# Attention heads in groups of two even and two odd ones, with their products issued in turn

## The chip, the cores and the metric

The program runs on one core of a Trainium2 chip. The metric is the device time of one execution in microseconds. A core has five engines with a queue of their own each: TensorE (PE, matmuls and transposes through a matmul with the identity; its weight loads are listed as PEld), VectorE (DVE), ScalarE (ACT), GpSimd (POOL) and SyncE (SP, which issues the weight loads from memory). An engine takes its instructions in the order in which the program issued them and waits on semaphores for the others.

## The reference

Two small models run one after the other on 256 tokens of 1024 channels. The first has two layers of a hybrid mixer (gated delta rule, retention, pooling) and a gated feed-forward. The second, with which this case deals, has two layers of a mixer with three attentions, a, b and c, and a feed-forward with squared relu. All heads are 64 wide, all arithmetic is float32.

```python
def hybrid_mixer_2(u, pos, w_in, idx_k_norm, sinks, w_a, w_b, w_c, w_o):
    (aq, ak, av, iq, ik, iw, bq, bk, bv, cq, ck, cv, gates) = split_columns(u @ w_in)
    ...
    o_a = dsa_attention(qa, ka, av, iqr, ikr, iw * IDX_HEADS ** -0.5)   # 6 heads, one k and v; 8 index heads
    o_b = dilated_attention(...)   # 4 heads in each of 3 groups; the softmaxes of the groups join
    o_c = sink_window_attention(..., sinks)   # 8 heads over 2 k and v heads, a sink logit in the softmax
    g = jax.nn.sigmoid(gates.reshape(Bsz, L, N_BRANCHES, D_MODEL))
    merged = (g[:, :, 0] * (o_a.reshape(Bsz, L, -1) @ w_a)
              + g[:, :, 1] * (o_b.reshape(Bsz, L, -1) @ w_b)
              + g[:, :, 2] * (o_c.reshape(Bsz, L, -1) @ w_c))
    return merged @ w_o
```

In attention a, 8 index heads give a score to each key, and only the best 64 keys of a row count.

## The kernel before

The tokens are two tiles of 128, t = 0 and t = 1. Tile 0 sees 128 keys, tile 1 sees 256 (`nk`).

**The main stream.** Products with weight matrices (`Block`, `unit`, `unit_b`, run by `run_blocks`) follow each other on PE in an order that is fixed when the program is built. Weights come by SP into `raw`; ACT copies them to `hi` (the part that the fast float32r format holds exactly), DVE subtracts to get `lo`, and each product is three matmuls: hi, lo and the rest of x with hi. Results go to four PSUM banks named `acc`; blocks that feed a feed-forward and all the small work use four others, named `sd`.

**The chains.** Everything else (norms, rope, attention) is written as Python generators, called chains. A chain yields the number of `sd` banks that its next step takes, or an event to wait for. While the program is built, the main stream calls `tick` after every few matmuls. A planner in the same code (`Engine.cost`, `mm`, `tr`, `op`) keeps an estimated clock for each engine, and lets a chain issue its next step when its operands are estimated to be ready. So the planner decides at which place of PE's order a chain's small products stand. On the chip the order is fixed, and a product whose operand is late holds up all that stands behind it on PE.

**The attentions.** `lane` (one chain for each token tile) runs `index_bias`, then the three attentions through `softmax_pv`. Queries and keys are transposed, two heads to a tile: an even head lies at partitions 0 to 63, an odd one at 64 to 127. The operands are `iqT`, `ikT` (index), `qaT`, `kaT` (a), `b1`, `b2`, `b3` (b), `c1`, `c2`, `ckT` (c); `av`, `bv1`, `bv2` and `cv` are the values. A unit is one head of b, or two heads of equal parity of a or c. `unit_pv` makes a unit's scores in a bank, DVE scales them and adds the mask into a tile `L`, finds the maximum `mx`; ACT takes the exponential and sums it into `den`; DVE divides; PE transposes `L` (128 columns at a time) and ACT copies the result to `PT`; then PE multiplies the values with `PT` into the attention's output bank, `po`: an even head at output partitions 0 to 63, an odd one at 64 to 127. `softmax_pv` takes up to two units of a token tile in flight: it waits for the unit before the last (`evs[-2]`) ahead of each new one. `split_T` then brings the output to `oT`, for the branch products of the main stream.

**In the order.** The units of the attentions before are `[[0, 2], [1, 3], [4], [5]]` for a, `[[0], [1], [2], [3]]` for b and `[[0, 2], [1, 3], [4, 6], [5, 7]]` for c. The products of a unit stand one behind the other, so those of one parity stand together.

Of the kernel before, what the change touches and what calls it, by code (L numbers as in the profile page):

```python
# [9 lines left out]
F32 = mybir.dt.float32  # L10
# [7 lines left out]
LEAD, RING = 8, 6  # L18
# [10 lines left out]
class Engine:  # L29
    """an engine's instructions, with an estimate of when each is done"""  # L30
# [43 lines left out]
class Chain:  # L74
    """g: generator; held: what its last step has yet to issue; r: what that step yielded; fin: when it is done"""
# [25 lines left out]
class Pair:  # L101
    """[128, 4, hi/lo, 256 tok] as two tiles of the arena"""
# [8 lines left out]
    def cuts(s, t, nk):  # L111
        """the first nk rows of token tile t, for split_T"""
        return [s.t[k // 2][:, 0:min(2, nk - k), :, t * 128:(t + 1) * 128] for k in range(0, nk, 2)]


class Net:
# [105 lines left out]
    def keys(s, a):  # L222
        """the parts of a tile, 128 elements each, that an access touches"""
# [6 lines left out]
    def when(s, ins, outs, lat=0.13):  # L230
        """when the operands of an instruction are ready"""
# [20 lines left out]
    def moved(s, t, mb, at=0.0):  # L252
        """a tile that a DMA fills, not before at"""
# [79 lines left out]
    def loads(s, n=3):  # L333
        """issue loads as far ahead as the buffers reach"""
# [13 lines left out]
    def hi(s, fine=False):  # L348
        """the high parts of the next piece, if there is room; fine: at most 512 columns of them"""
# [39 lines left out]
    def lo(s, fine=False):  # L389
        """the low parts of the next piece"""  # L390
# [20 lines left out]
    def hiready(s, fine=False):  # L411
        """when the high parts that the next low parts take are there"""
# [7 lines left out]
    def back(s, i):  # L420
        """how much work an engine may have before it when part of piece i is added"""
# [20 lines left out]
    def slack(s, i):  # L442
        """time that the tensor engine has to work before it takes piece i"""
# [20 lines left out]
    def unit(s, b, pi, t, half=None):  # L464
        """half: of the columns of kind "d", else both"""
# [90 lines left out]
    def ar(s, shape, name, dt=F32, kb=0):  # L556
        """a tile of the arena: slots of 1, 2 and 4 KiB a partition"""
# [50 lines left out]
    def rstd(s, parts, n):  # L608
        """(sum of the columns of parts / n + 1e-6) ** -0.5"""
# [14 lines left out]
    def split_T(s, cuts, ps):  # L624
        """the rows of ps [128, n, 128] in two parts; cuts: where they go, in [128, n, hi/lo, 128]"""
# [7 lines left out]
    def to_T(s, cuts, src):  # L633
        """transposes src [128 tok, nk*128], nk <= 4"""
# [9 lines left out]
    def norm_T(s, t, ss, w, ev):  # L644
        """xT of rms_norm(x[t]) * w; ss: sums of squares of the two halves"""
# [15 lines left out]
    def add_normed(s, t, acc, w, ns, ev):  # L661
        """x[t] += rms_norm(acc) * w, acc two banks, ev: the second is done; ns: sums of squares of the new x[t]"""
# [23 lines left out]
    def acc(s):  # L686
        """accumulators of kind "d", [t][half], taken when they are first used"""
# [148 lines left out]
class Mix1:  # L836
# [28 lines left out]
    def rope_tm(s, dst, src, cos, sin, nsin, nh, half):  # L865
        """dst, src [128, nh, 2, half]; tables [128, half]"""
# [8 lines left out]
    def branch_blocks(s, st, oT, ev, w, K, gt, first, done=None):  # L875
        """y += (1 + gt) * (o @ w), transposed: twice the gated sum; done: the split of y into xT"""
# [21 lines left out]
    def gate_blocks(s, w, c0, need):  # L898
        """tanh of half of 1024 columns (sigmoid is half of 1 + it), transposed; gt[half][pair of 128 columns]"""
# [17 lines left out]
    def out_bank(s, aT, v, q, sts):  # L917
        """[128 tok, head, dv]: a @ v plus each chunk's q @ (state before it)"""
# [29 lines left out]
    def decay(s, st, ba):  # L948
        """beta, running sums of the log decay and their exponentials"""
# [8 lines left out]
        # softplus(u) = max(u, 0) + log1p(exp(-|u|)); log1p(e) = 2 atanh(e / (2 + e))  # L958
# [33 lines left out]
    def conv(s, st, b):  # L992
        """evacuation of 128 transposed columns: causal convolution along the tokens, silu"""
# [17 lines left out]
    def delta(s, st, t):  # L1011
        """gated delta rule of one token tile (two chunks of 64), four heads side by side"""
# [10 lines left out]
        # inverse norms of the rows of q and k  # L1023
# [10 lines left out]
        # decay matrices  # L1034
# [32 lines left out]
        # attn^T  # L1067
# [11 lines left out]
        # (I + M)^-1 by doubling the diagonal blocks  # L1079
# [30 lines left out]
        # u and w^T  # L1110
# [48 lines left out]
        # attention inside the chunks, then what the states add  # L1159
# [131 lines left out]
    def mixer1(s, l, need, finish):  # L1291
        """blocks of one layer's mixer and what to do at its start"""
# [104 lines left out]
class Mix2:  # L1397
    def load_consts2(s):
# [4 lines left out]
        # cos and sin of position * inverse frequency, argument reduced to [-pi, pi]  # L1403
# [29 lines left out]
    def rope2(s, dst, src, t, nh):  # L1433
        """dst [128, nh*64] <- rope of src [128, nh*64]"""
# [4 lines left out]
    def tpairs(s, dst, t, src, n):  # L1439
        """dst[:, 0:n, tok t] <- transposes of n groups of 128 columns of src"""  # L1440
# [393 lines left out]
```

## Time and profile before

| | |
|---|---|
| median of 3 runs | 1920.66 us (1920.15 to 1921.56) |
| profiled execution, first to last instruction | 1918.9 us |
| PE busy | 1893.6 us (99%), 12498 matmul records |
| DVE busy | 1319.2 us (69%) |
| ACT busy | 1014.9 us (53%) |
| DMA | 313.52 MB, mean 163 GB/s |
| granted TensorE clock | 0.999 |

A busy share is that of the whole span. Matmuls are pipelined: the duration of one in the trace is longer than the distance to the next, so the distance between starts is what a product costs PE. A float32 product is two records. The views used are the page, the table of groups by line and form, the table by stretches of time, and the timeline of one engine; a line of the timeline merges neighbours of one kind and gives the start of the first, the time until the end of the last and the count.

### The profile page before, as it was taken

The page shows a single profiled execution, that of the slowest core. Times are in us where ns is not written, and L with a number is a line of the kernel's source. Part 1 is how long each engine was busy: PE and PEld are TensorE (multiplying, and loading weights), DVE is VectorE, ACT ScalarE, POOL GpSimd, SP SyncE. Part 2 cuts the span into 40 slices and gives each one's busy share as a digit, 9 for nine tenths or more (in the row PEclk, how much of TensorE's full clock was granted, in tenths as well). Part 3 has the DMA queues.
Part 4 walks back from the last instruction along what each step waited for, and adds up shares of the span by engine and source line. Part 5 has one row for each costly group of instructions (what it writes and reads, how often), then busy time and mean ns, then how long its engine had stood idle before and what let it go on. Part 6 is the DMA issues. An engine that isn't in the chain of part 4 may idle for free.

```text
span 1918.9 us, 31114 instructions
## 1 busy us (share of the span) xinstructions
PE 1893.6 (99%) x12498; PEld 1697.2 (88%) x12498; DVE 1319.2 (69%) x2616; ACT 1014.9 (53%) x1924; POOL 10.8 (1%) x23
## 2 busy tenths in 40 slices
PE   7999999999999999999999999999999999999998
PEld 6998897999899889889987789989998779998997
DVE  5787768655577786866558977675547887776552
ACT  6653456544575434655444556566544355556552
POOL 0000000000000000000000000000000000000000
PEclk9999999999999999999999999999999999999999
DMA  8542354765255325466524422556543332466540
GB/s 289 201 151 74 110 195 151 250 217 193 87 184 179 112 92 189 143 231 242 198 76 173 143 99 101 207 185 233 208 171 137 112 120 97 144 216 240 188 175 23
DMA packets 144336, 313.52 MB, mean 163 GB/s; under 512 B 5704, under 2 KB 20224, under 8 KB 144064
## 3 DMA queue, kind: packets, MB, share of 16 engines
q1 hardware_dynamic: 143376, 310.08, 46.5%
q0 software_dynamic: 816, 1.46, 0.3%
q8 instruction: 98, 1.61, 0.3%
q14 instruction: 46, 0.38, 0.1%
HBM read 310.47 MB, written 1.05 MB: 162 GB/s over the span
## 4 chain that ended last, share of the span: by engine, by line
PE 92%; DVE 3%; ACT 2%; DMA 1%; issue 1%; SPq 0%; DVEq 0%; ACTq 0%
PE acc L302 59%; PE sd L302 30%; PE sd L309 4%; ACT hi L49 1%; DVE lo L49 1%; DMA raw<-in_w_up_dram 1%; DMA raw<-in_ffn_gate_dram 0%; DVE rsb L49 0%; DMA row<-in_mix_pre_norm_dram 0%; ACT act L49 0%; ACT L49 0%; DVE rqx L49 0%; DVE xn L49 0%; DVE b L49 0%; ACT nsq L49 0%
## 5 line engine op out<-in xcount | busy, mean ns | idle before, releaser
L49 DVE TENSOR_TENSOR lo<-raw,hi 128x1024 fp32r<-128x1024 f32 (+3 forms) x703 | 687.2, 1014 | 232.4 <-ACT hi L49 194.1
L49 ACT ACTIVATE hi<-raw 128x1024 fp32r<-128x1024 f32 (+4 forms) x711 | 590.3, 877 | 164.9 <-PE acc L302 59.0
L302 PE MATMUL acc<-hi,xT 128*128 128x512 f32 (+3 forms) x1280 | 402.9, 384 | 2.7 <-ACT hi L49 1.6
L302 PE MATMUL acc<-xT,hi 128*128 128x256 f32 x1920 | 356.4, 285 | 0.0
L302 PE MATMUL sd<-xT,hi 128*128 128x256 f32 x1920 | 346.9, 283 | 0.0
L302 PEld LDWEIGHTS acc<-xT,hi 128*128 128x128 f32 x1920 | 296.2, 189 | 6.0 <-issue 3.9
L302 PEld LDWEIGHTS sd<-xT,hi 128*128 128x128 f32 x1920 | 296.2, 188 | 1.7
L302 PEld LDWEIGHTS acc<-hi,xT 128*128 128x128 f32 x1280 | 234.3, 189 | 50.7 <-issue 3.9
L302 PE MATMUL acc<-hi,actT 128*128 128x512 f32 x864 | 272.5, 391 | 0.0
L302 PE MATMUL acc<-xT,lo 128*128 128x256 f32 x960 | 270.8, 282 | 0.0
L302 PE MATMUL sd<-xT,lo 128*128 128x256 f32 x960 | 269.6, 281 | 0.0
L302 PE MATMUL acc<-lo,xT 128*128 128x512 f32 (+3 forms) x640 | 240.4, 376 | 1.2 <-DVE lo L49 1.2
L302 PEld LDWEIGHTS acc<-hi,actT 128*128 128x128 f32 x864 | 162.2, 188 | 33.1
L302 PEld LDWEIGHTS sd<-xT,lo 128*128 128x128 f32 x960 | 182.3, 190 | 0.0
L302 PEld LDWEIGHTS acc<-xT,lo 128*128 128x128 f32 x960 | 180.1, 188 | 0.0
L302 PE MATMUL acc<-lo,actT 128*128 128x512 f32 x432 | 168.5, 390 | 0.0
L302 PEld LDWEIGHTS acc<-lo,xT 128*128 128x128 f32 x640 | 121.3, 189 | 20.3 <-DVE lo L49 2.1
L302 PE MATMUL acc<-oT,hi 128*128 128x256 f32 x672 | 123.0, 284 | 0.0
L302 PEld LDWEIGHTS acc<-oT,hi 128*128 128x128 f32 x672 | 104.7, 191 | 0.3 <-issue 0.2
L302 PEld LDWEIGHTS acc<-lo,actT 128*128 128x128 f32 x432 | 81.1, 188 | 16.2
L49 DVE SCALAR_TENSOR_TENSOR actT<-actq,actT 128x256 fp32r<-128x256 f32 x84 | 34.3, 424 | 88.7 <-ACT actT L49 87.7
L302 PE MATMUL acc<-oT,lo 128*128 128x256 f32 x336 | 95.0, 283 | 0.0
(332 smaller groups left out, 2012.8 us busy)
## 6 DMA issues: line engine op xcount, KB each, us to landing
raw<-in_w_in_dram SPq DMA_DIRECT2D x110, 1024.0 KB, 5.1
raw<-in_w_up_dram SPq DMA_DIRECT2D x32, 1024.0 KB, 6.0
raw<-in_w_down_dram SPq DMA_DIRECT2D x32, 1024.0 KB, 4.9
raw<-in_ffn_down_dram SPq DMA_DIRECT2D x22, 1024.0 KB, 6.4
raw<-in_ffn_gate_dram SPq DMA_DIRECT2D x20, 1024.0 KB, 5.5
raw<-in_ffn_up_dram SPq DMA_DIRECT2D x20, 1024.0 KB, 5.1
raw<-in_w_out_dram SPq DMA_DIRECT2D x8, 1024.0 KB, 5.1
raw<-in_w_o_dram SPq DMA_DIRECT2D x8, 1024.0 KB, 5.2
```

The lines of the kernel that those rows point to most:

```text
L49: f(*a, **k)
L302: s.T.matmul(out, lhsT=l, rhs=r, start=start, stop=stop)
L309: s.T.transpose(out, a, s.ident if p == 128 else s.ident[0:p, 0:p])
```

## The change

The heads of an attention are taken in groups: `[[0, 1, 2, 3], [4, 5]]` for a, `[[0, 1], [2, 3]]` for b and `[[0, 1, 2, 3], [4, 5, 6, 7]]` for c. A group has one or two even heads and as many odd ones (`sides`). Each side has its own bank and its own tile `L`; the scores of the two sides are issued in turn, and so are the products with v. The small DVE instructions on `mx` and `den` cover all heads of a group. A group asks for two banks at once for its scores (`yield len(sides)`), of up to `cap` parts each. `softmax_pv` now waits for a group's end before it spawns the next one. The index scores of four heads are issued in turn into two banks. `rl` and the tiles `L` of 256 elements move to slots of 2 KiB. All other lines of the diff drop comments and docstrings.

```diff
-    def unit_pv(s, t, un, heads, po, sink, ev):
+    def unit_pv(s, t, grp, heads, po, sink, ev):
         V, S = s.V, s.S
         nk = 128 * (t + 1)
-        npart, per = len(heads[un[0]]), len(un)
-        parts = [p for h in un for p in heads[h]]
-        yield (len(parts) + 1) // 2
-        L = s.ar([128, len(parts), nk], "L")
-        for b in range(0, len(parts), 2):
-            bs = parts[b:b + 2]
-            ps = s.bank(True, [128, len(bs), nk])
-            for i, (qT, kT, mask, v) in enumerate(bs):
-                s.mm(ps[:, i], qT, kT[:, 0:nk])
...
+        sides = [u for u in ([h for h in grp if h % 2 == p] for p in range(2)) if u]
+        npart, per = len(heads[grp[0]]), len(sides[0])
+        n, cap, m = npart * per, 512 // nk, per * len(sides)
+        P = [[p for h in u for p in heads[h]] for u in sides]
+        Ls = [s.ar([128, n, nk], "L", kb=2 if n * nk <= 512 else 4) for u in sides]
+        for b in range(0, n, cap):
+            e = min(n, b + cap)
+            yield len(sides)
+            pss = [s.bank(True, [128, e - b, nk]) for u in sides]
+            for i in range(b, e):
+                for ps, parts in zip(pss, P):
+                    s.mm(ps[:, i - b], parts[i][0], parts[i][1][:, 0:nk])
...
+        V.tensor_scalar(mx[:, 0:m], mx[:, 0:m], -1.0, None, op0=ALU.mult)
+        for h, c, Li in at:
+            S.activation(Li, Li, AF.Exp, bias=mx[:, c:c + 1], accum_out=den[:, c:c + 1])
...
+        V.reciprocal(den[:, 0:m], den[:, 0:m])
+        for h, c, Li in at:
+            V.tensor_scalar(Li, Li, den[:, c:c + 1], None, op0=ALU.mult)
...
-        for i, h in enumerate(un):
-            mine = [x for x in blocks if x[0] // npart == i]
-            for n, (p, j) in enumerate(mine):
-                s.mm(po[64 * (h % 2):64 * (h % 2) + 64, h // 2], parts[p][3](j), PT[p, j], n == 0, n == len(mine) - 1)
+            mine = [(i * npart + p, j) for p in range(npart) for j in range(t + 1)]
+            for c, (x, j) in enumerate(mine):
+                for k, u in enumerate(sides):
+                    h = u[i]
+                    s.mm(po[64 * (h % 2):64 * (h % 2) + 64, h // 2], P[k][x][3](j), PT[k, x, j], c == 0, c == len(mine) - 1)
         s.fire(ev)
...
-        evs = []
-        for un in units:
-            if len(evs) > 1:
-                yield evs[-2]
-            evs.append(Ev())
-            s.spawn(s.unit_pv(t, un, heads, po, sink, evs[-1]))
-            yield 0
-        for ev in evs[-2:]:
+        for grp in groups:
+            ev = Ev()
+            s.spawn(s.unit_pv(t, grp, heads, po, sink, ev))
             yield ev
...
-        for hp in ((0, 2), (1, 3), (4, 6), (5, 7)):
-            ps = s.bank(True, [128, 2, nk])
-            for i, h in enumerate(hp):
...
+        for h0 in (0, 4):
+            hps = ((h0, h0 + 2), (h0 + 1, h0 + 3))
+            pss = [s.bank(True, [128, 2, nk]) for hp in hps]
+            for i in range(2):
+                for ps, hp in zip(pss, hps):
...
-        yield from s.softmax_pv(t, hs, [[0, 2], [1, 3], [4], [5]], st["oTa"], st["ev_oa"])
+        yield from s.softmax_pv(t, hs, [[0, 1, 2, 3], [4, 5]], st["oTa"], st["ev_oa"])
...
-        yield from s.softmax_pv(t, hs, [[0], [1], [2], [3]], st["oTb"], st["ev_ob"])
+        yield from s.softmax_pv(t, hs, [[0, 1], [2, 3]], st["oTb"], st["ev_ob"])
...
-        yield from s.softmax_pv(t, hs, [[0, 2], [1, 3], [4, 6], [5, 7]], st["oTc"], st["ev_oc"], st["sink"])
+        yield from s.softmax_pv(t, hs, [[0, 1, 2, 3], [4, 5, 6, 7]], st["oTc"], st["ev_oc"], st["sink"])
```

The planner places the steps anew, so the order on PE changes. In the rows that follow, a row is one product or several of a kind (x2), and the number behind a name tells one tile from the next.

PE, the first index scores of the second model's first layer, before: the two products of a bank (`sd_11039`) are two even heads of token tile 0, the next two even heads of tile 1.

```order
L302 MATMUL sd_11039<-ikT_10869,iqT_10623 128x128 x2
L302 MATMUL sd_11048<-ikT_10869,iqT_10623 128x256 x2
L302 MATMUL acc_10999<-hi_10792,xT_74 128x512
L302 MATMUL acc_10999<-lo_10793,xT_74 128x512
L302 MATMUL acc_10999<-hi_10792,xT_74 128x512
```

The same place now: even and odd heads alternate between two banks, and the two token tiles have main products between them.

```order
L302 MATMUL sd_11039<-ikT_10869,iqT_10623 128x128
L302 MATMUL sd_11040<-ikT_10869,iqT_10623 128x128
L302 MATMUL sd_11039<-ikT_10869,iqT_10623 128x128
L302 MATMUL sd_11040<-ikT_10869,iqT_10623 128x128
L302 MATMUL acc_10999<-hi_10792,xT_74 128x512
L302 MATMUL acc_10999<-lo_10793,xT_74 128x512
L302 MATMUL acc_10999<-hi_10792,xT_74 128x512
L302 MATMUL sd_11060<-ikT_10869,iqT_10623 128x256
```

Eight products that stood in four places now stand in two of each width.

PE, attention b of the same layer, before: products with v of one head of tile 1 (`sd_11816`), scores of one head of tile 1, products with v of one head of tile 0 (`sd_11751`), transposes of a tile `L`.

```order
L302 MATMUL sd_11816<-PT_12055,bv1_11375 64x128 x4
L302 MATMUL sd_11816<-PT_12060,bv2_11510 64x128 x2
L302 MATMUL sd_12087<-b2_11157,b1_10884 128x256
L302 MATMUL sd_12087<-b3_11269,b1_10884 128x256
L302 MATMUL sd_12091<-b3_11269,b2_11157 128x256
L302 MATMUL sd_11751<-PT_12076,bv1_11375 64x128 x2
L302 MATMUL sd_11751<-PT_12076,bv2_11510 64x128
L309 MATMUL sd_12101<-ident_75,L_12024 128x128 x3
```

And now, in the same attention: products with v of the first two heads of tile 0, in turn from two tiles `PT`, then the scores of its other two heads, in turn in two banks.

```order
L302 MATMUL sd_11820<-PT_11911,bv1_11369 64x128
L302 MATMUL sd_11820<-PT_11927,bv1_11369 64x128
L302 MATMUL sd_11820<-PT_11911,bv1_11369 64x128
L302 MATMUL sd_11820<-PT_11927,bv1_11369 64x128
L302 MATMUL sd_11820<-PT_11911,bv2_11488 64x128
L302 MATMUL sd_11820<-PT_11927,bv2_11488 64x128
L302 MATMUL sd_11955<-b2_11156,b1_10884 128x128
L302 MATMUL sd_11956<-b2_11156,b1_10884 128x128
L302 MATMUL sd_11955<-b3_11261,b1_10884 128x128
L302 MATMUL sd_11956<-b3_11261,b1_10884 128x128
L302 MATMUL sd_11955<-b3_11261,b2_11156 128x128
L302 MATMUL sd_11956<-b3_11261,b2_11156 128x128
```

What was one head's now alternates between an even and an odd head.

PE, the last products with v of attention c in the first layer, before: two units of tile 1, four products each, ahead of the last products of branch a (`oT_11712`).

```order
L309 MATMUL sd_12718<-ident_75,L_12588 128x128 x4
L302 MATMUL sd_12316<-PT_12701,cv_11735 64x128 x4
L302 MATMUL sd_12316<-PT_12723,cv_11735 64x128 x4
L302 MATMUL acc_12742<-oT_11712,hi_12499 128x256 x2
L302 MATMUL acc_12742<-oT_11712,lo_12500 128x256
```

And now: the eight alternate, and stand inside the gate products (`xT`) that follow branch a.

```order
L302 MATMUL acc_12735<-xT_74,lo_12511 128x256
L302 MATMUL sd_12369<-PT_12723,cv_11686 64x128
L302 MATMUL sd_12369<-PT_12747,cv_11686 64x128
L302 MATMUL sd_12369<-PT_12723,cv_11686 64x128
L302 MATMUL sd_12369<-PT_12747,cv_11686 64x128
L302 MATMUL sd_12369<-PT_12723,cv_11686 64x128
L302 MATMUL sd_12369<-PT_12747,cv_11686 64x128
L302 MATMUL sd_12369<-PT_12723,cv_11686 64x128
L302 MATMUL sd_12369<-PT_12747,cv_11686 64x128
L302 MATMUL acc_12734<-xT_74,hi_12510 128x256 x2
```

The end of the attentions has moved behind main products that it stood ahead of.

## Rows read from the trace of the kernel before

**Rows 1.** The page: span, PE's busy time, and the chain that ended last.
```profile
span 1918.9 us, 31114 instructions
...
PE 1893.6 (99%) x12498; PEld 1697.2 (88%) x12498; DVE 1319.2 (69%) x2616; ACT 1014.9 (53%) x1924; POOL 10.8 (1%) x23
...
PE 92%; DVE 3%; ACT 2%; DMA 1%; issue 1%; SPq 0%; DVEq 0%; ACTq 0%
```
**Rows 2.** Stretches of time: stretch, busy us of each engine, clock, DMA share, GB/s.
```profile
1036.00:1195.00 159.00, 158.51 (x988) 130.67 (x989) 129.21 (x335) 85.46 (x200) 0.00 (x0) 1.00 0.32 110
```
**Rows 3.** PE's groups by form: names, operand sizes, count, busy us, mean ns, idle.
```profile
L302 PE MATMUL sd<-b,b 64*128 64x256 f32 x48 | 12.5, 393 | 0.0
...
L302 PE MATMUL sd<-ikT,iqT 64*128 64x256 f32 x32 | 8.7, 392 | 0.0
...
L302 PE MATMUL sd<-ckT,c 64*128 64x256 f32 x32 | 6.7, 399 | 0.0
...
L302 PE MATMUL sd<-kaT,qaT 64*128 64x256 f32 x24 | 5.1, 411 | 0.0
```
**Rows 4.** The first layer's stretch, tile PT alone: PE, PEld and ACT.
```profile
1036.00:1195.00 159.00, 20.99 (x156) 15.92 (x156) 12.46 (x28) 1.00 0.32 110
```
**Rows 5.** PE's timeline around index scores: start, us, engine, line, out<-in, count.
```profile
1049.86 0.39 PE L302 MATMUL acc<-lo,xT 128*128 128x512 f32 x1
1050.09 0.40 PE L302 MATMUL acc<-hi,xT 128*128 128x512 f32 x1
1050.42 0.71 PE L302 MATMUL sd<-ikT,iqT 64*128 64x128 f32 x4
1051.06 0.51 PE L302 MATMUL acc<-hi,xT 128*128 128x512 f32 x1
1051.41 0.39 PE L302 MATMUL acc<-lo,xT 128*128 128x512 f32 x1
```
**Rows 6.** PE's timeline in attention b: scores alone, and products with v.
```profile
1119.31 0.93 PE L302 MATMUL sd<-b,b 64*128 64x128 f32 x6
1120.17 0.50 PE L302 MATMUL acc<-xT,hi 128*128 128x256 f32 x2
...
1125.77 0.87 PE L302 MATMUL sd<-PT,bv 128*64 128x128 f32 x6
1126.57 1.56 PE L302 MATMUL sd<-b,b 64*128 64x256 f32 x6
1128.06 0.87 PE L302 MATMUL sd<-PT,bv 128*64 128x128 f32 x6
```
**Rows 7.** PE's timeline in attention a: two units of unlike parity.
```profile
1084.72 0.72 PE L302 MATMUL sd<-kaT,qaT 64*128 64x128 f32 x8
1085.37 0.50 PE L302 MATMUL acc<-hi,xT 128*128 128x512 f32 x1
```
**Rows 8.** PE's timeline in the first model's delta rule: one half, then alternating halves.
```profile
230.15 1.09 PE L302 MATMUL sd<-S,kbe 128*64 128x128 f32 x8
231.17 0.50 PE L302 MATMUL acc<-xT,hi 128*128 128x256 f32 x2
...
232.79 1.09 PE L302 MATMUL sd<-S,qkv 128*64 128x128 f32 x16
233.81 1.16 PE L302 MATMUL sd<-vb,DT 128*128 128x128 f32 x8
```
**Rows 9.** PE's timeline at attention c's end.
```profile
1191.96 0.60 PE L309 MATMUL sd<-ident,L 128*128 128x128 f32 x4
1192.49 1.84 PE L302 MATMUL sd<-PT,cv 128*64 128x128 f32 x16
1194.27 0.50 PE L302 MATMUL acc<-oT,hi 128*128 128x256 f32 x2
```
**Rows 10.** DVE's timeline ahead of those transposes; a transpose of the second layer.
```profile
1190.90 0.61 DVE L49 TENSOR_SCALAR L<-L,den 128x256 f32<-128x256 f32 x2
...
1566.76 0.44 PE L309 MATMUL sd<-ident,L 128*128 128x128 f32 x2 [0.37 <-ACT PT L49]
```

More of the change, by code (lines that the diff above doesn't have):

```diff
@@ new lines, in unit_pv @@
+        sides = [u for u in ([h for h in grp if h % 2 == p] for p in range(2)) if u]
[10 more added lines that the diff above has]
+                    s.mm(ps[:, i - b], parts[i][0], parts[i][1][:, 0:nk])
+            for ps, parts, L in zip(pss, P, Ls):
+                for i in range(b, e, 2):
+                    j = min(e, i + 2)
+                    m0 = parts[i][2]
+                    mk = m0 if len(m0.shape) == 3 else m0[:, None, :].to_broadcast([128, j - i, nk])
+                    V.scalar_tensor_tensor(L[:, i:j], ps[:, i - b:j - b], 0.125, mk, op0=ALU.mult, op1=ALU.add)
@@ new lines, in unit_pv @@
+        mx = s.sm.tile([128, 4], F32, name="mx", tag="mx", bufs=4)
+        den = s.sm.tile([128, 4], F32, name="den", tag="den", bufs=4)
+        at = [(h, k * per + i, L[:, i * npart:(i + 1) * npart]) for k, (u, L) in enumerate(zip(sides, Ls)) for i, h in enumerate(u)]
+        for k, L in enumerate(Ls):
+            V.tensor_reduce(mx[:, k * per:(k + 1) * per], L.rearrange("p (a b) c -> p a (b c)", a=per), axis=AX.X, op=ALU.max)
+        if sink is not None:
+            for h, c, _ in at:
+                V.tensor_max(mx[:, c:c + 1], mx[:, c:c + 1], sink[:, h:h + 1])
@@ new lines, in unit_pv @@
+        V.tensor_scalar(mx[:, 0:m], mx[:, 0:m], -1.0, None, op0=ALU.mult)
+        for h, c, Li in at:
+            S.activation(Li, Li, AF.Exp, bias=mx[:, c:c + 1], accum_out=den[:, c:c + 1])
+        if sink is not None:
+            es = s.sm.tile([128, 4], F32, name="es", tag="es", bufs=4)
+            for h, c, _ in at:
+                S.activation(es[:, c:c + 1], sink[:, h:h + 1], AF.Exp, bias=mx[:, c:c + 1])
+            V.tensor_add(den[:, 0:m], den[:, 0:m], es[:, 0:m])
+        V.reciprocal(den[:, 0:m], den[:, 0:m])
@@ new lines, in unit_pv @@
+        for h, c, Li in at:
+            V.tensor_scalar(Li, Li, den[:, c:c + 1], None, op0=ALU.mult)
+        PT = {}
+        for k, L in enumerate(Ls):
+            blocks = [(i, j) for i in range(n) for j in range(t + 1)]
+            yield (len(blocks) + 3) // 4
+            for b in range(0, len(blocks), 4):
+                bl = blocks[b:b + 4]
+                pt = s.bank(True)
+                for c, (i, j) in enumerate(bl):
+                    s.tr(pt[:, c * 128:(c + 1) * 128], L[:, i, j * 128:(j + 1) * 128])
+                sb = s.ar([128, 512], "PT")
+                S.activation(sb[:, :len(bl) * 128], pt[:, :len(bl) * 128], AF.Copy)
+                for c, (i, j) in enumerate(bl):
+                    PT[k, i, j] = sb[:, c * 128:(c + 1) * 128]
@@ L1497, in unit_pv, with softmax_pv @@
+        yield 0
+        for i in range(per):
+            mine = [(i * npart + p, j) for p in range(npart) for j in range(t + 1)]
[3 more added lines that the diff above has]
+                    s.mm(po[64 * (h % 2):64 * (h % 2) + 64, h // 2], P[k][x][3](j), PT[k, x, j], c == 0, c == len(mine) - 1)
         s.fire(ev)
-    def softmax_pv(s, t, heads, units, oT, evo, sink=None):
+    def softmax_pv(s, t, heads, groups, oT, evo, sink=None):
@@ L1504, in softmax_pv @@
         po = s.bank(True, [128, nh // 2, 128])
-        evs = []
-        for un in units:
-            if len(evs) > 1:
-                yield evs[-2]
-            evs.append(Ev())
-            s.spawn(s.unit_pv(t, un, heads, po, sink, evs[-1]))
-            yield 0
-        for ev in evs[-2:]:
+        for grp in groups:
+            ev = Ev()
+            s.spawn(s.unit_pv(t, grp, heads, po, sink, ev))
             yield ev
@@ L1523, in index_bias @@
         yield st["ev_iq"][t]
-        yield 1
+        yield 2
         nk = 128 * (t + 1)
@@ L1528, in index_bias @@
         sc, s2 = s.ar([128, nk], "sc"), s.ar([128, nk], "s2")
-        for hp in ((0, 2), (1, 3), (4, 6), (5, 7)):
-            ps = s.bank(True, [128, 2, nk])
-            for i, h in enumerate(hp):
-                r = slice(64 * (h % 2), 64 * (h % 2) + 64)
-                s.mm(ps[:, i], iqT[r, h // 2, t * 128:(t + 1) * 128], ikT[r, 0, 0:nk])
-            rl = s.ar([128, 2, nk], "rl")
-            S.activation(rl, ps, AF.Relu, scale=0.125)
-            for i, h in enumerate(hp):
-                V.scalar_tensor_tensor(sc, rl[:, i], iw[:, t, h:h + 1], cm if h == 0 else sc, op0=ALU.mult, op1=ALU.add)
-            yield 1
+        for h0 in (0, 4):
[3 more added lines that the diff above has]
+                for ps, hp in zip(pss, hps):
+                    h = hp[i]
+                    r = slice(64 * (h % 2), 64 * (h % 2) + 64)
+                    s.mm(ps[:, i], iqT[r, h // 2, t * 128:(t + 1) * 128], ikT[r, 0, 0:nk])
+            for ps, hp in zip(pss, hps):
+                rl = s.ar([128, 2, nk], "rl", kb=2)
+                S.activation(rl, ps, AF.Relu, scale=0.125)
+                for i, h in enumerate(hp):
+                    V.scalar_tensor_tensor(sc, rl[:, i], iw[:, t, h:h + 1], cm if h == 0 else sc, op0=ALU.mult, op1=ALU.add)
+            yield 2 if h0 == 0 else 0
         cur, oth = sc, s2
```

31 lines of the change are left out of this document (removed).

## Prediction

> **What bounds the kernel now.** I read the page's head first, then its chain, then the first attention stretch, then the tensor engine's timeline inside them. The head shows TensorE (PE) busy 99% of a span of 1918.9 us, and the chain that ended last is PE for 92% [rows 1]. So time taken out of PE's stream is worth its full length, unless PE then waits for somebody. The change touches the two mixers of the second model, whose attentions lie at about 1036 to 1195 us in the first layer and come once more, alike, in the second. In the first stretch PE is busy 158.5 of 159 us, VectorE (DVE) 129.2 and ScalarE (ACT) 85.5, at full granted clock [rows 2]. The main products of xT with the weights run there without a break, and the attentions' small matmuls are cut into them. Those small matmuls are the only thing on the path that the change can shorten.
>
> **The products concerned.** Each float32 product stands in the trace as two records. The scores contract over 64 partitions (even heads lower half, odd heads upper half). In both layers they have 32 (index), 24 (a), 48 (b) and 32 (c) records of 256 columns [rows 3], and the 128-column forms have the same counts: 136 of each width. The products with v write 64 output partitions, 156 records a layer, 312 in all [rows 4].
>
> **Price of one, alone.** Four records of 128 columns take 0.64 us from their start to the next product's (1050.42 to 1051.06) [rows 5]; six take 0.86, and six of 256 columns 1.49 [rows 6]. So a record costs 0.11 or 0.215 us, and a run of them about 0.20 us on top. The products with v: six take 0.80 us [rows 6], eight of the like shape in the first model 1.02 [rows 8]: 0.11 each, and 0.15 on top. Beside this each stretch of small products slows its neighbours: the 512-column product ahead takes 0.33 us instead of 0.23, the one behind 0.35 [rows 5], together 0.2.
> Alone, all of it is 136 x 0.11 + 136 x 0.215 + 312 x 0.11 = 15.0 + 29.2 + 34.3 = 78.5 us.
>
> **What issuing in turn is worth.** Two rows tell. Before, unit [0,2] and unit [1,3] of the first attention can stand back to back: that stretch's eight records take 0.65 us, as long as four of one parity [rows 7, 5]. So matmuls on the two halves of the rows overlap fully. For halves of the output columns: in the delta rule sixteen records that alternate between the two chunks take 1.02 us, as long as eight that do not [rows 8]. Without alternation it does not come: sixteen products with v, eight of one parity and then eight of the other, take 1.78 us, one record less than 16 x 0.11 + 0.15 = 1.91 [rows 9]. So b's and the index scores (no overlap now) and all products with v go to half, and a's and c's scores only in part, since eight of their stretches are such pairs already. These eight (four of each width) save 4 x 4 x 0.11 + 4 x 4 x 0.215 = 5.2 us today. Left to win: 78.5 / 2 - 5.2 = 34 us.
> The Trainium skill, TensorE: Matmul & The Clock Gate, Part 3, "The mechanism", says that matmuls start and end strictly in program order. By that the pair of units in rows 7, issued even, even, odd, odd, would be serial and take twice as long; the measured 0.65 us disagrees, and the measurement decides. With the rule the sum would be 5 us larger, at about 1881.
>
> **Fewer changes of form.** By the program's order the 63 stretches of small products become 45, the runs of one form inside them 49 to 36 for scores and 39 to 22 for products with v. 18 x 0.20 + 13 x 0.20 + 17 x 0.15 = 8.8 us. I take 3 off, since a border between two parities in one stretch already hides a record, as in rows 9, some twenty to thirty times. Sum so far: 34 + 9 - 3 = 40 us. The bounds of this sum: 36 (another four lost where a group's second half waits for its tile) to 43 (nothing lost at the borders).
>
> **What else moves.** Weight loads (SP's queue) and their order do not change. DVE loses 72 small instructions (reciprocals, negations, sums now for four heads at once), ACT none; DVE and ACT have no part of the end of the chain, so I cost that at nothing. Their large instructions keep shape and number. The softmax of a group now takes two units' DVE and ACT work in sequence, and a token tile has one group under way, no longer two units.
>
> **Waits that may come.** PE issues in order: behind a transpose that waits for its softmax stand the main products. Today the margin is small: the transposes at 1191.96 [rows 9] start 0.45 us after DVE scaled their tile (1190.90 + 0.61) [rows 10], and one transpose did wait, 0.37 us for ACT to clear its bank [rows 10]. Faster small products eat this margin. Against that, the planner, which places each step by estimated costs, gave the longer groups more main products to hide behind: by the order, c's last products with v now stand 84 main products of 256 columns later, and their reader, c's branch product, still another 270 behind, so the end of the attentions holds nobody up. Between no wait at all and 0.8 us (0.45 + 0.37) for each of the 24 groups (six per token tile and layer), that is 0 to 19 us, I take 0.2 us a group, half of the one wait that a row shows: 5 us.
> DVE has to fit: 129 us of work a layer in a stretch that shrinks from 159 to about 141, 92%, so I do not expect it to be the bound, but it is the first candidate.
>
> **Sum.** 40 - 5 = 35 us off the profiled execution: 1918.9 - 35 = 1884. The median of the runs is 1920.66, 1.8 us more than the span, which lies outside the first and last instruction. Predicted: 1886 us.
>
> **Rivals.**
> *The chain of a group becomes the limit.* Two units in flight hid each other's softmax; one group does not. For it: margins of half a microsecond. Against: two token tiles still run side by side. At 0.8 us a group 19 us go back: 40 - 19 = 21, 1900.
> *The products with v do not overlap* (their two heads write one bank, and wait for different transposed tiles). For it: rows 9. Against: the delta rule's alternating halves do write one bank [rows 8]. Their half, 17 us, is lost: 40 - 17 - 5 = 18, 1903.
> *Nothing overlaps in the new order.* Only the changes of form remain, 9 - 5 = 4 us: 1917, no change. Against it speak rows 7 and 8 together.
> *Slower: PSUM banks.* There are four side banks, and each token tile's attention keeps one for its output. A group asks for two at once, so one group's scores take all that is left and the other tile's transposes stand in PE's queue until DVE has added the masks. There are 42 such askings a layer, 84 in all. At the 0.37 us of rows 10 each, 31 us go back (1912); from 0.48 us on the kernel is slower, and at 0.7 us it is 84 x 0.7 - 40 = 19 us slower, 1940. Against it: before, a b unit asked for two banks too.
> The Trainium skill names this in TensorEngine Tiling (Array Packing), "Gotcha 1: PSUM Pressure": row tiles need different banks at the same time; the trace agrees only in that one wait of 0.37 us.
>
> **How the numbers follow.** Forecast 1886 with a chance of 0.67, its own range 1879 to 1893; chain of a group 0.16; products with v not overlapped 0.08; nothing overlaps 0.05; banks 0.04. The range for 8 in 10 takes in the first three cases' middles: from a gain of 42 without waits (1878.5) to the 18 of the third (1903): 1878 to 1904. About 0.2%, 4 us, can be told from no change. Faster: the first three, 0.91; same: the fourth, 0.05; slower: the last, 0.04.
>
> **What would show it.** In the changed profile: a stretch of eight index records of 128 columns takes about 0.65 us, twelve of b about 0.86 (not 1.5), twelve products with v about 0.8 (not 1.5), if the steps are right. The distance from the first index score to the last product with v, less the main products in it, tells the waits: idle time of PE ahead of transposes, or a first transposed product late by more than its neighbours, are the 5 us. The main products keep 0.23 us. I am wrong if small stretches stay at their old length per record, if PE shows idle ahead of transposes or scores for more than 15 us in both layers, or if the weight splits come late after 1195 (PE waiting for lo).

## The result and the profile after

The changed kernel takes 1888.14 us (median of 4 runs, 1887.70 to 1889.96), the kernel before beside it 1921.11 us (1920.15 to 1921.57): a ratio of 0.9828 with a 95% interval of 0.9815 to 0.9841. The gain is 33.0 us where 34.7 were forecast. The page's head and the shares of its chain, which answer to [rows 1]:

```profile
span 1888.2 us, 31067 instructions
...
PE 1860.3 (99%) x12498; PEld 1673.0 (89%) x12498; DVE 1303.0 (69%) x2544; ACT 1011.8 (54%) x1924; POOL 10.8 (1%) x23
...
PE 92%; DVE 3%; ACT 3%; DMA 1%; issue 1%; SPq 0%; DVEq 0%
```

PE has as many records as before and 33 us less busy time, and it is still 92% of the chain. DVE has the 72 small instructions fewer that were forecast, and did not become the bound: in the stretch of [rows 2] it is busy for 132 of 159 us.

Next, PE's timeline of the changed kernel at four places: index scores, products with v of b, scores of b, and the end of attention c (start, us, engine, line, names, operand sizes, form, count). The distance from a row's start to the next row's is what a group costs.

```profile
1042.13 0.71 PE L302 MATMUL sd<-ikT,iqT 64*128 64x128 f32 x8
1042.77 0.51 PE L302 MATMUL acc<-hi,xT 128*128 128x512 f32 x1
...
1568.14 0.88 PE L302 MATMUL sd<-PT,bv 128*64 128x128 f32 x12
1568.95 0.88 PE L309 MATMUL sd<-ident,L 128*128 128x128 f32 x6
...
1571.18 0.94 PE L302 MATMUL sd<-b,b 64*128 64x128 f32 x12
1572.05 0.50 PE L302 MATMUL acc<-xT,hi 128*128 128x256 f32 x2
...
1189.49 1.09 PE L302 MATMUL sd<-PT,cv 128*64 128x128 f32 x16
1190.52 0.51 PE L302 MATMUL acc<-xT,hi 128*128 128x256 f32 x2
```

Counted in records, of which a product has two: eight index records take 0.64 us, as long as four did [rows 5]; twelve with v 0.81, as long as six [rows 6]; twelve score records of b 0.87, as long as six [rows 6]; sixteen with cv 1.03, where [rows 9] have 1.78. So each form overlaps in full.

Two sums run through the rest. **Stages:** between the first transposes of the normed rows (`sd<-ident,xn`) of one stage and of the next, the second model's two mixers took 273.92 + 275.73 = 549.65 us before and take 256.26 + 257.42 = 513.68 now. **Stretches:** for each stretch of small products inside them, the distance from the start of the main product ahead to the start of the second one behind, less what these two take among their like. Before, 63 stretches cost 97.8 us; now 45 cost 60.0. So the stretches give 37.8 us, and the stages keep 36.0 of it: 1.8 us net went to the time between stretches, mostly to waits. Two new waits stand in attention a; the bracket gives PE's idle time and what ended it:

```profile
1109.26 0.33 PE L309 MATMUL sd<-ident,L 128*128 128x128 f32 x1 [0.58 <-DVE L L49]
...
1111.04 0.43 PE L302 MATMUL sd<-PT,av 128*64 128x128 f32 x2
1111.90 0.43 PE L302 MATMUL sd<-PT,av 128*64 128x128 f32 x2 [0.43 <-ACT PT L49]
```

Of the 36.0 us, 3.7 were lost again in the profiled execution, ahead of the change: the first model's two feed-forward stages took 192.09 and 192.14 us where before had 190.22 and 190.36. Their instructions are the same. The row by stretches (busy us of the engines, then the granted clock) shows why, first the changed kernel's first execution, then another execution of the same kernel:

```profile
320.00:332.00 12.00, 10.65 (x45) 8.16 (x44) 10.02 (x21) 7.74 (x14) 0.00 (x0) 0.89 0.38 114
```
```profile
320.00:332.00 12.00, 10.70 (x51) 8.09 (x50) 10.23 (x22) 7.92 (x15) 0.00 (x0) 1.00 0.35 100
```

The mean granted clock is 0.89 in the one and 1.00 in the other, at the same share of busy time, and fewer products fit into the 12 us. A part of the stretch therefore ran at the lower level, 1.2 GHz.

Behind the change 1.2 us more were lost: the last stage takes 197.61 us where before had 196.37. Nearly all of it is the last write to memory, first before, then the changed kernel (start, us, the engine that issues it):

```profile
1914.89 0.99 SPq L1801 DMA_DIRECT2D out_dram<-fin  x2
```
```profile
1883.05 0.99 SPq L1812 DMA_DIRECT2D out_dram<-fin  x2
```

From its issue to the end of the span (1918.9 and 1888.2) there are 4.0 us before and 5.1 now. All three profiles of the unaltered changed kernel have 5.1; what makes the difference is open.

### The profile page after: what moved, and what is told of

Read it like the earlier page. It is cut to its first block, busy times and chain, and to the rows that moved or that the text cites. A ratio compares the mean times of both kernels' runs of the same rounds, so it can differ in the third digit from the quotient of the medians.

```text
span 1888.2 us, 31067 instructions
## 1 busy us (share of the span) xinstructions
PE 1860.3 (99%) x12498; PEld 1673.0 (89%) x12498; DVE 1303.0 (69%) x2544; ACT 1011.8 (54%) x1924; POOL 10.8 (1%) x23
## 4 chain that ended last, share of the span: by engine, by line
PE 92%; DVE 3%; ACT 3%; DMA 1%; issue 1%; SPq 0%; DVEq 0%
PE acc L302 60%; PE sd L302 28%; PE sd L309 4%; ACT hi L49 1%; DMA raw<-in_w_up_dram 1%; DVE lo L49 1%; DMA raw<-in_ffn_gate_dram 0%; ACT L49 0%; DMA row<-in_mix_pre_norm_dram 0%; ACT act L49 0%; ACT L L49 0%; DVE rsb L49 0%; DVE rqx L49 0%; DVE b L49 0%; DVE L L49 0%
## 5 line engine op out<-in xcount | busy, mean ns | idle before, releaser
L49 ACT ACTIVATE actq<-sd 128x256 f32<-128x256 f32 x84 | 31.3, 380 | 119.7 <-PE sd L302 119.7
```

Of the source, the lines that this page charges most:

```text
L49: f(*a, **k)
```

## The experiments

All are edits of the changed kernel, except where the text says otherwise. Each was timed beside the kernel before on the same chip (medians there 1922.24, 1921.56 and 1922.05 us for the three groups of runs).

| run | median us | ratio to before, interval | mixer stages, us | stretches, us |
|---|---|---|---|---|
| (before, first profile) | 1921.11 | 1 | 549.65 | 97.8 |
| (changed, first profile) | 1888.14 | 0.9828 [0.9815, 0.9841] | 513.68 | 60.0 |
| e1_no_turn | 1896.61 | 0.9866 [0.9851, 0.9881] | 522.00 | 69.1 |
| e2_pv_no_turn | 1895.97 | 0.9862 [0.9847, 0.9877] | 520.53 | 67.7 |
| e3_scores_no_turn | 1886.45 | 0.9815 [0.9800, 0.9830] | 514.74 | 61.6 |
| e4_groups_in_flight | 1893.69 | 0.9854 [0.9838, 0.9871] | 520.78 | 64.9 |
| e5_index_only | 1916.22 | 0.9971 [0.9960, 0.9982] | 544.38 | 89.8 |
| e7_groups_of_one_parity | 1933.90 | 1.0065 [1.0050, 1.0080] | 561.59 | 106.9 |
| e8_turns_of_two | 1887.19 | 0.9818 [0.9801, 0.9834] | 514.10 | 60.5 |
| e9_after_again | 1886.92 | 0.9819 [0.9804, 0.9833] | 513.74 | 60.0 |
| e10_whole_attentions | 1880.80 | 0.9784 [0.9771, 0.9798] | 508.26 | 55.9 |
| e6_retention_in_turn | 1883.29 | 0.9796 [0.9783, 0.9809] | 513.90 | 60.0 |
| e11_both | 1878.72 | 0.9772 [0.9759, 0.9785] | 508.55 | 55.8 |
| e12_after_control | 1887.78 | 0.9820 [0.9807, 0.9834] | 513.65 | 60.0 |

**e1_no_turn.** The groups stay, but inside each one side's products stand ahead of the other's, in the index, the scores and the products with v.
```diff
-            for i in range(b, e):
-                for ps, parts in zip(pss, P):
+            for ps, parts in zip(pss, P):
+                for i in range(b, e):
```


> The changed kernel with its groups, banks and tiles, but all products of the even heads ahead of those of the odd ones, for the index scores, the scores and the products with v. Theory (the gain is the overlap of two halves of the array, and the products with v overlap only if issued in turn): products with v go back to one at a time but for one record at each border of the two sides, 312 x 0.11 / 2 - 24 x 0.11 = 14.5 us; scores of four records a side keep overlapping as the pair of units did before, b's of six records a side partly lose it, 0 to 3 us. 1888 + 14.5 to 17.5 = 1903 to 1906. Rival 1 (the gain comes from the groups: fewer stretches, fewer small instructions, other places): about 1888, unchanged. Rival 2 (neither kind overlaps without turns): 14.5 + 34 - 17 = 31 us, 1919.

Measured 1896.61, between the theory and its first rival. Of the 37.8 us that the stretches gained, 28.7 stay without any turn (97.8 - 69.1). Only 9.1 us hang on the order inside a group.

**e2_pv_no_turn and e3_scores_no_turn.** The same edit for the products with v alone, and for the index and the scores alone.

> The changed kernel, only the products with v issued side after side. Theory: 14.5 us slower than the changed kernel, 1902.6; a stretch of twelve records of b takes 1.35 to 1.45 us instead of 0.8. Rival (overlap does not need turns): 1888.

> The changed kernel, only the index scores and the scores issued side after side, two banks as before. Theory: eight records, four a side, still overlap, as in attention a before: 0 to 3 us slower, 1888 to 1891, and b's twelve records of 128 columns (six a side) tell how many the array's queue looks past: 0.86 us if all, about 1.0 if four. Rival (scores overlap only in turn): 136 x 0.055 + 136 x 0.108 = 22 us less what the border hides, 1907 to 1910.

The 9.1 us split into 7.7 for the products with v (67.7 - 60.0) and 1.6 for the scores (61.6 - 60.0). The median of e3, 1886.45, shows no loss at all and lies below its theory's 1888 to 1891; beside the unaltered kernel's 1886.92 (e9) only the stretches and stages tell the small cost. e2's theory fell, as e1's did: side after side, the products with v do overlap, but only at the border of the two sides. First e2 (twelve records of one side, then twelve of the other), then the changed kernel (the same 24 in turn):

```profile
1135.40 2.45 PE L302 MATMUL sd<-PT,bv 128*64 128x128 f32 x24
1137.79 0.55 PE L309 MATMUL sd<-ident,L 128*128 128x128 f32 x3
```
```profile
1136.54 1.53 PE L302 MATMUL sd<-PT,bv 128*64 128x128 f32 x24
1138.01 0.55 PE L309 MATMUL sd<-ident,L 128*128 128x128 f32 x3
```

In turn they take 1.47 us. Wholly in sequence they would take twelve records more, 1.47 + 12 x 0.11 = 2.79. e2 takes 2.39: 0.40 us, or between three and four records, are hidden. By the same sum over the stretches, sixteen hide 3.6 records (1.701 us against 1.214 in turn), twelve hide 3.2 (1.265 in e1 against 0.958), and eight, four of each side, hide all four (0.738 against 0.730). The scores do likewise. In e3 six of b and then six take 1.19 us, where in turn it was 0.87 and in sequence 0.87 + 0.66 = 1.53, which is three records hidden:

```profile
1114.89 1.26 PE L302 MATMUL sd<-b,b 64*128 64x128 f32 x12
1116.08 0.50 PE L302 MATMUL acc<-xT,hi 128*128 128x256 f32 x2
```

So in these rows PE starts the other half's products three to four records early, in stretches of eight to twenty-four records alike. Most score groups here have four records a side, and need no turn at all. One row of e2 shows the overtaking itself. In the program's order, all 24 records with bv stand ahead of the eight with cv; by the starts in PE's timeline the first three of cv begin among the last three of bv:

```profile
1157.35 2.13 PE L302 MATMUL sd<-PT,bv 128*64 128x128 f32 x21
1159.21 0.32 PE L302 MATMUL sd<-PT,cv 128*64 128x128 f32 x1
1159.31 0.27 PE L302 MATMUL sd<-PT,bv 128*64 128x128 f32 x1
1159.37 0.27 PE L302 MATMUL sd<-PT,cv 128*64 128x128 f32 x1
1159.42 0.27 PE L302 MATMUL sd<-PT,bv 128*64 128x128 f32 x1
1159.47 0.27 PE L302 MATMUL sd<-PT,cv 128*64 128x128 f32 x1
1159.53 0.27 PE L302 MATMUL sd<-PT,bv 128*64 128x128 f32 x1
1159.58 0.65 PE L302 MATMUL sd<-PT,cv 128*64 128x128 f32 x5
```

**e8_turns_of_two.** The sides change after two products (four records) instead of one.
```diff
-            for c, (x, j) in enumerate(mine):
+            for c0 in range(0, len(mine), 2):
                 for k, u in enumerate(sides):
                     h = u[i]
+                    for c, (x, j) in list(enumerate(mine))[c0:c0 + 2]:
```


> The changed kernel, but the products with v change sides after every two products (four records) instead of after every one. Theory (TensorE looks about four records past a waiting one): the two sides overlap nearly as fully as with single turns, mixer phases of 256 to 258 us, 1885 to 1891. Rival (only strict turns of one product overlap, and each change of sides hides just a fixed piece): like side after side, mixer phases of 259 to 261 us, 1894 to 1897.

The theory held: stretches 60.5 against 60.0, stages 514.10 against 513.74. Runs of four records are short enough.

**e7_groups_of_one_parity.** The new code and its one group under way for each token tile, but with the groups and index scores of the kernel before.
```diff
-        yield from s.softmax_pv(t, hs, [[0, 1], [2, 3]], st["oTb"], st["ev_ob"])
+        yield from s.softmax_pv(t, hs, [[0], [1], [2], [3]], st["oTb"], st["ev_ob"])
```


> The changed code (one group under way for each token tile, batched reciprocals and negations), but with the groups of the kernel before: one parity in each, and its index scores. Theory (all of the gain comes from opposite halves side by side): no gain is left, and the eight score stretches that stood in pairs by chance lose their overlap, 5 us: 1922 to 1930. Rival (part of the gain is from the batched small instructions of VectorE or from the planner's new places): 1900 to 1915.

1933.90, worse than the kernel before, and by 4 us more than the upper end expected. There are 69 stretches that cost 106.9 us, 9.1 more than before: the chance pairs of [rows 7] are gone, and there are six stretches more. The rest of the 11.9 us in the stages, 2.8, is mostly waits: PE is idle for 3.5 us in the two stages where it was 1.4 before. So the new code and new places in the order bring no gain as such. The batching over four heads is not tested by e7: with its small groups DVE has 2600 instructions, only 16 fewer than before. But nothing is left for it to explain, since the stretches on PE alone gave more (37.8 us) than the stages gained (36.0).

**e5_index_only.** The kernel before with only its index scores in groups of four.

> The kernel before with one part of the change alone: the index scores of two even and two odd heads in turn, everything else as before. Theory (the gain is the overlap of the two row halves plus fewer stretches): half of 32 records of 0.11 us and of 32 of 0.215 us, 5.2 us, plus eight stretches fewer at about 0.3 us, so 7 to 8 us off the kernel before, about 1914. Rival (the gain comes only when a whole attention's groups are reordered, through the planner): within 2 us of the kernel before, about 1921.

The stretches gave 8.0 us (97.8 - 89.8), as expected, but the stages only 5.3. PE, earlier now, twice met a main product that waits until ACT has emptied a gate's bank, once in each layer, 2.7 us together, which is the difference:

```profile
1191.98 0.50 PE L302 MATMUL acc<-oT,hi 128*128 128x256 f32 x2 [1.31 <-ACT gt L49]
...
1580.32 0.51 PE L302 MATMUL acc<-xT,hi 128*128 128x256 f32 x2 [1.39 <-ACT gt L49]
```

**e4_groups_in_flight.** All groups of an attention are started at once, as a test of whether one group under way costs waits.
```diff
-            ev = Ev()
-            s.spawn(s.unit_pv(t, grp, heads, po, sink, ev))
-            yield ev
+            evs.append(Ev())
+            s.spawn(s.unit_pv(t, grp, heads, po, sink, evs[-1]))
+            yield 0
+        for ev in evs:
+            yield ev
```


> The changed kernel, but a token tile's groups of one attention are all spawned at once, instead of one after the other's end. Theory (what is left of waits on PE in the attentions is about 2 us in both layers, so the chain of a group is no limit): 1886 to 1889. Rival (one group in flight costs PE the 5 us that the forecast took): 1883. Rival (banks: two groups of a tile and two tiles ask for two banks each where two are free): slower, 1890 to 1897.

Slower by 5.6 us than the first result of the changed kernel, inside the range of the third expectation (banks), and all of it in the second layer: its stage takes 265.69 us against 257.42, the first layer's 255.09 against 256.26. There PE waits for DVE and ACT, and its clock falls behind the waits:

```profile
1555.21 0.55 PE L309 MATMUL sd<-ident,L 128*128 128x128 f32 x3 [0.72 <-DVE L L49]
1556.67 0.55 PE L309 MATMUL sd<-ident,L 128*128 128x128 f32 x3 [0.91 <-DVE L L49]
...
1560.76 1.54 PE L302 MATMUL sd<-PT,bv 128*64 128x128 f32 x10 [1.34 <-ACT PT L49]
```
```profile
1540.00:1560.00 20.00, 16.54 (x119) 12.53 (x118) 15.51 (x41) 8.62 (x21) 0.00 (x0) 0.94 0.28 93
1560.00:1580.00 20.00, 19.24 (x149) 16.45 (x150) 15.30 (x40) 9.44 (x20) 0.00 (x0) 0.89 0.21 61
```

DVE's row beside the first two tells what they waited for:

```profile
1554.74 0.75 DVE L49 TENSOR_SCALAR L<-L,den 128x384 f32<-128x384 f32 x2
1555.40 0.61 DVE L49 TENSOR_TENSOR rpa<-acc,cb 128x192 f32<-128x192 f32 x2
1555.93 1.28 DVE L49 SCALAR_TENSOR_TENSOR L<-sd,cb 128x512 f32<-128x512 f32 x2
```

The wait of 0.72 us ends as DVE has scaled a tile. That of 0.91 us does not: every tile was scaled by 1555.49, and the transposes start at 1556.67, when DVE has read the first of two score banks. By the program's order they write that bank. So the bank rival holds in part, and operands that came late are the rest.

PE is idle for 3.5 of 20 us, and in this stretch and the next the mean clock is 0.94 and 0.89, so a part of each ran at 1.2 GHz. All groups at once do not help.

**e9_after_again and e12_after_control.** The changed kernel, unaltered.

> The changed kernel again, unaltered, to see whether the fall of the granted clock in the first model's two feed-forwards (1.8 us each in its first profile) belongs to the kernel or to the execution. If to the execution: feed-forward phases of 190.4 to 192.2 us that differ from the first profile's, and a median between 1884 and 1889. If to the kernel: 192.1 us in both again, and 1888.

> The changed kernel unaltered, as the measure for the three above on the same chip: 1886 to 1889, by whether the granted clock falls in the first model's feed-forwards.

The feed-forward stages took 190.44 and 190.51 us in e9, 190.49 and 190.59 in e12, and the mixers again 513.7. So the fall of the clock belongs to an execution, not to the kernel. Other runs show it in one of the two stages (e2: 190.41 and 192.18; e10: 190.46 and 192.25).

**Three versions that go further.** e10 makes one group of a's six heads and one of c's eight (`[[0, 1, 2, 3, 4, 5]]`, `[[0, 1, 2, 3, 4, 5, 6, 7]]`). e6 treats the first model's retention alike:
```diff
+        if t == 0:
+            yield 2
+            pvs = [s.b4() for r in range(2)]
+            for h in H:
+                for r, pv in enumerate(pvs):
+                    rows = slice(r * 64, r * 64 + 64)
+                    s.mm(pv[:, h], kz[rows, h], v[rows, h])
```


> The changed kernel with larger groups: attention a's six heads in one group, attention c's eight in one, b's as changed. Theory (what a group saves beyond the overlap is the change of form around each stretch, about 0.4 us a score stretch and 0.34 us a stretch of products with v): some sixteen of each fewer in both layers, less those that stood in one stretch anyway, 4 to 8 us off the changed kernel, 1879 to 1883. Rival (a longer softmax between scores and products is no longer hidden): waits of TensorE ahead of transposed tiles eat it, 1886 to 1895.

> The changed kernel, and the same treatment for the first model's retention: the state products of the two chunks of token tile 0 (eight records of 64 rows each, 1.28 us each today) are issued in turn into two banks. Theory: the second eight are hidden, about 1.3 us in each of two layers, 2.6 us off the changed kernel, 1884. Rival (the later first state update and the two banks asked for at once hold up the chain of the retention): no gain, 1887 or more.

> Both additions in one kernel: retention in turn, and one group for each of the attentions a and c. Theory: the gains add, 1876 to 1881. Rival: as the worse of the two alone, 1887 to 1893.

e10 is 7.0 us faster than the unaltered kernel on the same chip: 39 stretches instead of 45 cost 4.1 us less, and the stages are 5.4 us shorter; its last write takes 4.0 us, 1.1 less. The waits of the rival did not come. A stretch of 32 records with cv takes 1.90 us, 0.06 a record:

```profile
1183.16 1.97 PE L302 MATMUL sd<-PT,cv 128*64 128x128 f32 x32
1185.06 0.50 PE L302 MATMUL acc<-xT,hi 128*128 128x256 f32 x2
```

e6 is 4.5 us faster. Its two first mixer stages are shorter by 1.4 and 1.5 us (300.93 against 302.32, 298.19 against 299.68), a little over the 2.6 expected together; the remainder lies before and after the stages (0.5 us at the start, and 1.1 in the last write, which takes 4.0 us here) and is no effect that I can place. The row shows sixteen records of 64 rows in 1.09 us, where the changed kernel takes 1.08 for the first eight alone:

```profile
184.65 1.16 PE L302 MATMUL sd<-rv,rk 64*128 64x128 f32 x16
185.74 1.16 PE L302 MATMUL sd<-B,R 128*128 128x128 f32 x8
```
```profile
182.68 1.16 PE L302 MATMUL sd<-rv,rk 64*128 64x128 f32 x8
183.76 1.16 PE L302 MATMUL sd<-Tm,MT 128*128 128x128 f32 x8
```

e11, both together, is the fastest: 1878.72 us, 9.1 less than the unaltered kernel, 0.9772 of the kernel before (0.9759 to 0.9785). The medians of the two alone add up to 11.5, but the 1.1 us of the last write stand in the profiles of both; e11's stages are shorter by 7.7 (1.2 + 1.5 in the first model, 5.1 in the second), and its last write takes 4.0 us. It lies inside the range expected.

## Why the prediction was right, and where its steps were not

**The bound.** Right. Time taken out of PE's stream was worth its full length: 37.8 us out of the stretches made the two stages 36.0 us shorter, and e7, with the new code and no overlap, gained nothing. That DVE and ACT have no part of the chain's end misreads [rows 1], which give them 3% and 2%; nothing came of it.

**Price of a record, and the overlap.** Right, for both kinds of halves. The prices of [rows 5, 6, 8] gave 34 us for the halving; the three groups named as tests came at 0.64, 0.81 and 0.87 us, where 0.65, 0.8 and 0.86 were said. The sum of 40 us, with the changes of form in it, measured 37.8. Of the missing 2.2 us one row has 0.85: the stretch at 1111.04 that waited for ACT's copy cost 1.42 us, where a like stretch costs 0.57 (the profile calls 0.43 of it idle). The rest, 1.3 us, I can't place.

**"Without alternation it does not come."** Wrong, and it is the step that failed. I took the 1.78 us of [rows 9] for a property of PE. ACT's row of the kernel before, beside it, has the reason (the bracket is ACT's own wait for the transposes):

```profile
1192.60 0.60 ACT L49 ACTIVATE PT<-sd 128x512 f32<-128x512 f32 x1 [1.21 <-PE sd L309]
```

The odd unit's `PT` was not there until 1193.20. Eight records from then on, by the price of the prediction, last 8 x 0.11 + 0.15 = 1.03 us, until 1194.23, and the next product starts at 1194.27 [rows 9]. So the late operand accounts for the end of that row, whether halves overlap or not, and the row could not tell. Two other rows of the kernel before could. By the program's order they have twelve records of one half and then six of the other, and eight and then four:

```profile
1610.90 1.80 PE L302 MATMUL sd<-PT,bv 128*64 128x128 f32 x18
1612.63 0.88 PE L309 MATMUL sd<-ident,L 128*128 128x128 f32 x6
...
1651.01 1.20 PE L302 MATMUL sd<-PT,cv 128*64 128x128 f32 x12
1652.14 0.51 PE L302 MATMUL acc<-xT,hi 128*128 128x256 f32 x2
```

They take 1.73 and 1.13 us where the prediction's price gives 2.13 and 1.47 in sequence: 0.40 and 0.34 us, three to four records, are hidden without any turn. The 3 us that the sum took off for borders came near only by luck: the order before has five borders of the two halves between products with v, not twenty to thirty, and hides three to four records where no operand is late, instead of one: about 2 us at 0.11 us a record.

So the order inside a group was worth 9.1 us, and putting opposite parities beside each other, with fewer stretches, 28.7. The forecast did not suffer, because the changed kernel has both; the rival in which the products with v do not overlap would have deserved less chance.

In e2 PE starts products out of the program's order, as the rows from 1159.21 on show; what stands ahead of the prediction on the order of an engine's instructions does not hold for these starts. The Trainium skill, TensorE: Matmul & The Clock Gate, Part 3, "The mechanism", has matmuls starting and ending strictly in program order; the starts in those rows disagree, and so does the full overlap of four and four.

**Waits.** Right in kind, too large: 5 us (0.2 a group) were put down, half of one observed wait. Net 1.8 us came outside the stretches, and 0.85 inside one. e5 shows that such waits needn't be in the attentions: a main product behind a gate cost it 2.7 us.

**The rivals.** The chain of a group did not become the limit, and e4 shows that the opposite, more groups in flight, does harm. The rival of the banks was there, at a small price. The wait of 0.58 us at 1109.26 is one for a bank:

```profile
1108.39 0.48 DVE L49 TENSOR_SCALAR L<-L,den 128x128 f32<-128x128 f32 x2
1108.79 0.75 DVE L49 SCALAR_TENSOR_TENSOR L<-sd,bias 128x256 f32<-128x256 f32 x2
```

DVE had scaled both tiles by 1108.87. The transposes started only when DVE's next instruction had read scores out of a bank to add their mask, and by the program's order that is the bank that the transposes write. The 0.19 us at 1115.31, until ACT emptied a bank (`c`), are the only other such wait of the changed kernel's attentions. The rival's count was too high as well: of its 42 askings a layer only 18 are for two score banks; the other 24 are for transposes, and all but four of these ask for one bank.

**The remaining 2 us.** The forecast was 1886; the medians of the unaltered kernel were 1888.14, 1886.92 and 1887.78. Two things, neither foreseen, are of that size. One is the clock's fall ahead of the change, 1.6 to 1.9 us for each stage in which it comes. The granted clock of the timed runs goes with their time: of the unaltered kernel's twelve runs, five at 0.999 took 1886.69 to 1887.07 us, six at 0.998 took 1887.70 to 1889.12, and one at 0.997 took 1889.96. The other is the last write, 1.1 us, in every profile of the unaltered kernel. That the two make up the whole difference is not shown.

## What to carry to other kernels

Where products use half the rows or half the columns of the array, put the two halves beside each other in PE's order; with up to four records a side any order will do, beyond that take turns. Count stretches as well as products: by the prices of the prediction a stretch of one form costs 0.35 to 0.4 us beyond its records here (0.15 or 0.20 of its own and 0.2 on its neighbours), so larger groups gain again (e10). No run here tells at what size a longer softmax shows as waits. And when two rows seem to show that an engine can't overlap, look first at when the second one's operand was ready.

## What the runs showed of the hardware

- PE starts matmuls of one half of the array while three to four records of the other half, earlier in the program, have yet to start (1.701, 1.265 and 2.53 us for stretches of 16, 12 and 24 records that would take 2.09, 1.62 and 2.93 in sequence; 1159.21 in e2 for the starts).
- The granted clock can fall in one execution and not in the next, with the same instructions: 0.89 against 1.00 in twelve microseconds of which PE is idle for 1.3 in both, worth about 1.6 us a stage between executions of one kernel. What decides it is open.
- In e4 the clock fell behind waits that left PE idle for 3.5 of 20 us. The stage was 8.3 us longer than the changed kernel's, and PE was idle for 3.9 us more in it. The rest is the clock and four more stretches, in shares that no run tells apart.
